# Pooling's doubling sums moved from GpSimd to VectorE, and the pooling units taken in reversed order

## The chip, the cores and the metric

The kernel runs on one core of a Trainium2 chip. The metric is the device time of one execution in microseconds (us). Lower is better. The engines are named as the profile names them: PE (TensorE's matmuls), PEld (TensorE's weight loads), DVE (VectorE), ACT (ScalarE), POOL (GpSimd), SP (SyncE, which issues DMAs).

## What is computed

One decoder layer, sequence 2048, width 1024, fp32. Two branches share one input projection `w_in` (six groups of 1024 columns: q, k, v, a gate, u, a second gate). The retention branch has 8 heads of 128. The pooling branch is a causal moving mean of u over a window, minus u itself, then a linear map per group, a scale and a gate. The 1024 pooled channels are four groups of 256 with windows 2, 4, 8 and 16:

```python
cs = jnp.cumsum(uf, axis=1)
for g, w in enumerate(POOL_WINDOWS):          # 2, 4, 8, 16
    cg = cs[..., sl]
    shifted = jnp.pad(cg, ((0, 0), (w, 0), (0, 0)))[:, :s]
    count = jnp.minimum(t + 1.0, float(w))[None, :, None]
    mixed = (cg - shifted) / count - uf[..., sl]
    outs.append(jnp.einsum('bsc,cd->bsd', mixed, pool_w[g]))
y_pool = concat(outs) * pool_scale * silu(g_pool)
```

Both branches are concatenated, mapped by `w_out`, normalised and added to x.

## The kernel before, in words

**Tiling.** Every large product is a 2x2 block product done the Strassen way, with seven products in place of eight. A "unit" is one such 2x2 problem with blocks of 128 output channels by 512 tokens. Each of its seven products is 12 matmuls of 128x512 (four slices of the contraction, three terms each, since operands are split into a rounded high part and a rest: `split`, L144 on ACT and L145 on DVE). The order of the products is 6, 2, 5, 7, then product 1 of the next unit, 4, 3. Three PSUM banks (a, b, c) hold the sums; bank b takes products 6, 7 and 4 in turn, and DVE or ACT must have read the bank after one of them before the next may add to it. So product 7 waits for the readers of product 6 (L340 on DVE, then the copy u at L315 on ACT), and product 4 waits for the reader of product 7 (L348 on DVE, called gp in a pooling unit).

**Phases.** `line` lists the units of four phases. Phase 0 does token blocks 0 and 1, phase 1 blocks 2 and 3; each has 24 units: a qk and a vg unit for each of the 8 heads and 8 pooling units `up0` to `up7` (two for each window: `g = f // 2`). `mixer_units` (L803) puts one pooling unit behind each head from head `lead` on (3 in phase 0, 2 in phase 1), and what is left at the end of the phase. Phases 2 and 3 are the output projection, 8 units each, first on the heads' half and then on the pooled half. At the end of a phase, `Resident.fetch` loads the next phase's moving operand and splits it: 14 copies `rh` of 128x1024 on ACT and 14 subtractions `rl` on DVE, within the last unit or two.

**Order of work.** The main loop emits one product, runs its readers (`uses`), then `slot()`, which runs what earlier stages have put there with `later(i, stage)` (i products ahead), then the chores of that point (`chores`, L1098), and the splits for the next unit (`prep`). The tile framework then orders each engine's instructions by its own plan; every engine runs its queue in order.

**The pooling unit** (`pool_unit`, L591). Product 2 gives u of the first block, 7 the gate of the second block, 4 the gate of the first, 3 u of the second. `values` writes u behind 16 columns of history into `ub`; `gate` applies SiLU on ACT. As soon as both are there (after product 4 for the first block, after product 3 for the second), `mix` runs whole: doubling sums (L631) on GpSimd, each adding a tile to itself shifted by 1, 2, 4, 8 (one sum for window 2, up to four for window 16), then on DVE the mean minus u (L634), for block 0 the first 16 columns once more (L638, L640), the scale and gate (L642), and a store by a DMA that GpSimd issues (`put_y`, L450). All this is emitted in the slot of the product that gave the last input.

`chores` also calls `fold_pool_weights(g)`, which multiplies the pooling weights of group g into the projection before the units of that group need them.

Of the kernel before, what the change touches and what calls it, by code (L numbers as in the profile page):

```python
# [13 lines left out]
ALU = mybir.AluOpType  # L14
# [4 lines left out]
KT = DM // P  # L19
KH = KT // 2  # L20
BLK = 512
# [8 lines left out]
HIST = 16  # L30
# [6 lines left out]
C_ID, C_TRI, C_G2, C_EPS, C_CNT, C_INVF, C_SGN, C_HPI = 0, 128, 256, 264, 272, 336, 337, 338  # L37
# [44 lines left out]
def layer_kernel(ctx: ExitStack, tc: tile.TileContext, x, xt, pos, wt, wut, wo, pw, cols, postg, const, out):  # L82
    nc = tc.nc
# [13 lines left out]
    cst = kp.tile([P, C_W], F32, name="cst")  # L97
    col = kp.tile([P, 3 * KT], F32, name="col")
# [20 lines left out]
    def T(name):  # L119
        return tmp.tile([P, BLK + HIST], F32, name=name, tag="t", bufs=NT)  # L120
# [34 lines left out]
    def later(i, stage):  # L155
        while len(slots) <= i:
            slots.append([])
        slots[i].append(stage)
# [290 lines left out]
    def put_y(b, f, t):  # L449
        nc.gpsimd.dma_start(out=yd[b][:, :, f, :], in_=t.rearrange("p (c t) -> p c t", c=CPB))  # L450
# [86 lines left out]
    def w_quads(f1, f2):  # L537
        lo, hi = slice(0, BLK), slice(BLK, 2 * BLK)
        return {"11": f1[:, lo], "12": f1[:, hi], "21": f2[:, lo], "22": f2[:, hi]}
# [54 lines left out]
    def pool_unit(f, b0, b1):  # L594
        g = f // 2
        win, E = WINDOWS[g], BLK + HIST
        sg, ub = {}, {}

        def gate(b):
            def use(c, i):  # L600
                t = T(f"gp{f}_{b}")[:, :BLK]
                if not i:
                    c(t)
                    c = t
                nc.scalar.activation(out=t, in_=c, func=AF.Silu)
                sg[b] = t
                mix(b)
            return use

        def values(b):  # L610
            def use(c, i):
                u = T(f"ub{f}_{b}")
                nc.scalar.copy(out=u[:, :HIST], in_=hist[f])
                if i:
                    nc.scalar.copy(out=u[:, HIST:], in_=c)
                else:
                    c(u[:, HIST:])
                nc.scalar.copy(out=hist[f], in_=u[:, BLK:])
                ub[b] = u
                mix(b)  # L620
            return use

        def mix(b):
            if b not in sg or b not in ub:
                return
            n, u = f"{f}_{b}", ub[b]
            src, step = u, 1
            while step < win:
                dst = T(f"w{n}_{step}")
                s0 = 2 * step - 1  # L630
                nc.gpsimd.tensor_tensor(out=dst[:, s0:], in0=src[:, s0:], in1=src[:, s0 - step:E - step], op=ALU.add)  # L631
                src, step = dst, 2 * step
            mx = T(f"mx{n}")[:, :BLK]
            nc.vector.scalar_tensor_tensor(out=mx, in0=src[:, HIST:], scalar=1.0 / win, in1=u[:, HIST:],  # L634
                                           op0=ALU.mult, op1=ALU.subtract)
            if b == 0:
                c0 = C_CNT + g * HIST
                nc.vector.tensor_tensor(out=mx[:, :HIST], in0=src[:, HIST:2 * HIST], in1=cst[:, c0:c0 + HIST],  # L638
                                        op=ALU.mult)
                nc.vector.tensor_tensor(out=mx[:, :HIST], in0=mx[:, :HIST], in1=u[:, HIST:2 * HIST],  # L640
                                        op=ALU.subtract)
            nc.vector.scalar_tensor_tensor(out=mx, in0=mx, scalar=col[:, 2 * KT + f:2 * KT + f + 1], in1=sg[b],  # L642
                                           op0=ALU.mult, op1=ALU.mult)
            put_y(b, KT + f, mx)

        return Unit(f"up{f}_{b0}", w_quads(wf[f], wt[4 * HEADS + f]),
                    {"11": values(b0), "12": values(b1), "21": gate(b0), "22": gate(b1)})
# [90 lines left out]
    def load_fold(g, dh):  # L738
        return [landing(f"wr{g}{dh}{ct}", wut[2 * g + dh][:, ct * BLK:(ct + 1) * BLK]) for ct in range(2)]

    def load_pool(g):
        return landing(f"pr{g}", pw[g])

    def halves(name, val):
        hi, lo = (T(f"{name}{k}")[:, :BLK] for k in "hl")
        split(hi, lo, val)
        return hi, lo

    def fold_split(g, dh, raw):
        return [halves(f"w{g}{dh}{ct}", raw[ct]) for ct in range(2)]  # L750

    def fold_products(g, dh, pool, w):
        phi, plo = pool
        sums = []
        for kk in range(2):
            o = rps(f"wf{g}_{dh}{kk}")
            for e in range(2):
                for ct in range(2):
                    whi, wlo = w[ct]
                    d0 = (2 * kk + e) * P  # L760
                    ds = slice(d0, d0 + P)
                    cs = slice(ct * 256, (ct + 1) * 256)
                    oe = o[:, e * 256:(e + 1) * 256]
                    nc.tensor.matmul(oe, r32(whi[:, ds]), r32(phi[:, cs]), start=(ct == 0), stop=False)
                    nc.tensor.matmul(oe, r32(whi[:, ds]), r32(plo[:, cs]), start=False, stop=False)
                    nc.tensor.matmul(oe, r32(wlo[:, ds]), r32(phi[:, cs]), start=False, stop=(ct == 1))
            sums.append(o)
        return sums

    def fold_store(g, dh, sums):  # L770
        fold = [T(f"wf{g}{j}{dh}")[:, :BLK] for j in range(2)]
        for kk, o in enumerate(sums):
            for j in range(2):
                nc.scalar.copy(out=fold[j][:, kk * 256:(kk + 1) * 256].rearrange("p (e c) -> p e c", e=2),
                               in_=o.rearrange("p (e c) -> p e c", e=2)[:, :, j * P:(j + 1) * P])
        for j in range(2):
            nc.gpsimd.dma_start(out=wf[2 * g + j][:, dh * BLK:(dh + 1) * BLK], in_=fold[j])

    def fold_pool_weights(g):
        st = {"pr": load_pool(g), 0: load_fold(g, 0)}  # L780

        def begin():
            st["p"] = halves(f"p{g}", st["pr"])

        def operands(dh):
            st[dh] = fold_split(g, dh, st[dh])

        def multiply(dh):
            st[dh] = fold_products(g, dh, st["p"], st[dh])

        def second():
            st[1] = load_fold(g, 1)
        later(2, begin)
        later(3, lambda: operands(0))
        later(6, lambda: multiply(0))
        later(7, lambda: fold_store(g, 0, st[0]))
        later(7, second)
        later(10, lambda: operands(1))
        later(13, lambda: multiply(1))
        later(14, lambda: fold_store(g, 1, st[1]))  # L800


    def mixer_units(b0, b1, lead):  # L803

        units = []
        pool = [pool_unit(f, b0, b1) for f in range(KT)]
        for h in range(HEADS):
            units += head_units(h, b0, b1)
            if h >= lead:
                units.append(pool.pop(0))  # L810
        return units + pool
# [259 lines left out]
    def stats_next(b):  # L1071
        ss = sml.tile([P, 2 * CPB], F32, name=f"ss{b}", tag="ss2", bufs=2)

        def rows(st):
            for j in range(2):
                t = T(f"xs{b}_{st}{j}")[:, :BLK]
                nc.sync.dma_start(out=t, in_=x[b * BLK + st * P:b * BLK + (st + 1) * P, j * BLK:(j + 1) * BLK])
                later(3, lambda t=t, j=j: nc.scalar.activation(out=t, in_=t, func=AF.Square,
                                                               accum_out=ss[:, 2 * st + j:2 * st + j + 1]))
        for st in range(CPB):  # L1080
            later(st, lambda st=st: rows(st))

        def scales():
            v = sml.tile([P, CPB], F32, name=f"rs{b}", tag="rs")
            s2 = ss.rearrange("p (s j) -> p s j", j=2)
            nc.vector.tensor_tensor(out=v, in0=s2[:, :, 0], in1=s2[:, :, 1], op=ALU.add)
            dg = diagonals(b, scale_h(b, v))
            later(2, lambda: spread_h(b, dg, True))
        later(9, scales)

    def postg_tiles():
        for j, tag in enumerate(("cos", "sin")):
# [2 lines left out]
            pg.append(t)  # L1095


    chores = {(0, 4, 0): lambda: fold_pool_weights(0), (0, 10, 0): lambda: fold_pool_weights(1),  # L1098
              (0, 14, 3): lambda: fold_pool_weights(2), (0, 16, 4): lambda: fold_pool_weights(3),
              (0, 6, 0): lambda: stats_next(2), (0, 7, 3): lambda: stats_next(3),  # L1100
              (0, 12, 1): lambda: tables(2), (0, 13, 2): lambda: tables(3),
              (0, last[0], 0): lambda: fetch_tables(2), (0, last[0], 1): lambda: fetch_tables(3),
# [9 lines left out]
    for n, (ph, i, u) in enumerate(line):  # L1112
# [5 lines left out]
        if after:  # L1118
            src = sources(ph + 1)
# [57 lines left out]
```

## Time and profile before

| | |
|---|---|
| median of 3 runs | 1507.88 us (1505.86 to 1511.87) |
| profiled execution, own time | 1509.98 us |
| profiled execution, span of the trace | 1508.0 us |
| mean granted TensorE clock | 0.985 |
| busy PE / DVE / ACT / POOL | 1436.5 / 1077.0 / 709.6 / 349.3 us |

Busy time is the sum over instructions of an engine; what it was not busy it waited. Stretches are given in us from the start of the span. Phase 0 ends and phase 1 begins at about 610 us, phase 1 gives way to phase 2 at about 1175 us, phase 2 to phase 3 at about 1330 us. "tail" below means the last pooling units of a phase, which stand one behind another.

### The profile page before, as it was taken

The page shows a single profiled execution, that of the slowest core. Times are in us where ns is not written, and L with a number is a line of the kernel's source. Part 1 is how long each engine was busy: PE and PEld are TensorE (multiplying, and loading weights), DVE is VectorE, ACT ScalarE, POOL GpSimd, SP SyncE. Part 2 cuts the span into 40 slices and gives each one's busy share as a digit, 9 for nine tenths or more (in the row PEclk, how much of TensorE's full clock was granted, in tenths as well). Part 3 has the DMA queues.
Part 4 walks back from the last instruction along what each step waited for, and adds up shares of the span by engine and source line. Part 5 has one row for each costly group of instructions (what it writes and reads, how often), then busy time and mean ns, then how long its engine had stood idle before and what let it go on. Part 6 is the DMA issues. An engine that isn't in the chain of part 4 may idle for free.

```text
span 1508.0 us, 20797 instructions
## 1 busy us (share of the span) xinstructions
PE 1436.5 (95%) x6976; PEld 1194.8 (79%) x6976; DVE 1077.0 (71%) x2280; ACT 709.6 (47%) x1353; POOL 349.3 (23%) x415
## 2 busy tenths in 40 slices
PE   5999999999999998999999999999998899998985
PEld 3888888888888876788888888888876788877874
DVE  7997677867866778776776768676767544576766
ACT  6464565555554434545444444443445433453321
POOL 0001012121302255310121213123135322112222
PEclk9999999999999999999999999999999999999998
DMA  8134365544545775643545635554537655798976
GB/s 335 32 95 123 107 177 149 162 139 107 159 114 152 226 219 184 204 112 92 147 139 140 162 96 156 138 152 137 155 86 224 202 152 153 220 289 212 235 219 166
DMA packets 115372, 243.79 MB, mean 162 GB/s; under 512 B 14016, under 2 KB 14144, under 8 KB 115264
## 3 DMA queue, kind: packets, MB, share of 16 engines
q1 hardware_dynamic: 79296, 156.46, 31.9%
q0 software_dynamic: 35968, 86.00, 25.3%
q8 instruction: 54, 0.88, 0.3%
q14 instruction: 54, 0.44, 0.1%
HBM read 187.88 MB, written 54.53 MB: 161 GB/s over the span
## 4 chain that ended last, share of the span: by engine, by line
PE 44%; DVE 5%; issue 5%; DMA 4%; POOL 3%; ACT 1%; SPq 1%; POOLq 0%; DVEq 0%; ACTq 0%
POOL w L631 2%; DMA S_o<-yd 2%; PE b_o L330 2%; PE b_o L331 2%; PE b_up L330 2%; PE b_o L332 2%; PE b_up L331 2%; PE b_up L332 2%; PE b_vg L332 1%; PE b_vg L330 1%; PE b_vg L331 1%; PE b_qk L330 1%; PE b_qk L331 1%; PE b_qk L332 1%; PE c_o L330 1%
## 5 line engine op out<-in xcount | busy, mean ns | idle before, releaser
L330 PE MATMUL b_up<-rh,h_up 128*128 128x512 f32 x192 | 78.6, 409 | 13.5 <-DVE gp L348 8.3
L330 PE MATMUL b_o<-rh,h_o 128*128 128x512 f32 x192 | 78.2, 407 | 13.5 <-DVE ot_o L348 9.2
L450 POOL DMA_DIRECT2D yd<-sg x32 | 24.7, 770 | 237.8 <-DVE sg L531 160.2
L331 PE MATMUL b_o<-rl,h_o 128*128 128x512 f32 x192 | 77.3, 403 | 0.0
L332 PE MATMUL b_up<-rh,l_up 128*128 128x512 f32 x192 | 77.0, 401 | 0.0
L331 PE MATMUL b_up<-rl,h_up 128*128 128x512 f32 x192 | 77.0, 401 | 0.0
L332 PE MATMUL b_o<-rh,l_o 128*128 128x512 f32 x192 | 76.9, 401 | 0.0
L330 PE MATMUL b_qk<-rh,h_qk 128*128 128x512 f32 x180 | 71.7, 398 | 3.1 <-ACT u_qk L315 2.5
L524 ACT ACTIVATE on<-op,sh,y_o 128x128 f32<-128x128 f32 x128 | 48.2, 457 | 51.5 <-DVE sh L521 51.5
L330 PE MATMUL b_vg<-rh,h_vg 128*128 128x512 f32 x180 | 72.0, 400 | 0.0
L331 PE MATMUL b_qk<-rl,h_qk 128*128 128x512 f32 x180 | 70.5, 392 | 0.8 <-DVE rl L145 0.6
L332 PE MATMUL b_qk<-rh,l_qk 128*128 128x512 f32 x180 | 70.4, 391 | 0.1
L331 PE MATMUL b_vg<-rl,h_vg 128*128 128x512 f32 x180 | 70.4, 391 | 0.0
L332 PE MATMUL b_vg<-rh,l_vg 128*128 128x512 f32 x180 | 70.4, 391 | 0.0
L263 POOL DMA_DIRECT2D S_qk<-in_wt x30 | 26.5, 907 | 174.0 <-DMA S_qk<-in_wt 114.6
L145 DVE TENSOR_TENSOR rl<-m,rh 128x1024 fp32r<-128x1024 f32 x42 | 53.0, 1265 | 19.1 <-ACT rh L144 16.4
L631 POOL TENSOR_TENSOR w<-w 128x525 f32<-128x525 f32 (+2 forms) x48 | 63.6, 1324 | 5.9 <-issue 2.8
L330 PEld LDWEIGHTS b_up<-rh,h_up 128*128 128x128 f32 x192 | 37.3, 194 | 24.5 <-DVE gp L348 10.0
L263 POOL DMA_DIRECT2D S_vg<-in_wt x30 | 26.6, 910 | 129.9 <-DMA S_vg<-in_wt 54.2
L330 PEld LDWEIGHTS b_o<-rh,h_o 128*128 128x128 f32 x192 | 37.5, 195 | 24.2 <-DVE ot_o L348 11.1
L330 PE MATMUL a_o<-rh,h_o 128*128 128x512 f32 x128 | 49.9, 390 | 2.8 <-ACT x_o L338 2.8
L631 POOL TENSOR_TENSOR w<-ub 128x527 f32<-128x527 f32 x32 | 44.0, 1374 | 35.9 <-DVE ub L354 15.2
(498 smaller groups left out, 4675.5 us busy)
## 6 DMA issues: line engine op xcount, KB each, us to landing
m<-made SPq DMA_DIRECT2D x30, 512.0 KB, 5.5
made<-c POOLq DMA_DIRECT2D x48, 256.0 KB, 3.3
yd<-sg POOLq DMA_DIRECT2D x32, 256.0 KB, 2.7
S_up<-in_wt POOLq DMA_DIRECT2D x32, 256.0 KB, 6.1
yd<-mx POOLq DMA_DIRECT2D x32, 256.0 KB, 2.9
b<-in_wo SPq DMA_DIRECT2D x32, 256.0 KB, 4.0
S_o<-yd SPq DMA_DIRECT2D x32, 256.0 KB, 3.4
S_o<-yd POOLq DMA_DIRECT2D x32, 256.0 KB, 7.2
```

What stands on the lines that cost most here:

```text
L145: (eng or nc.vector).tensor_tensor(out=r32(lo), in0=val, in1=hi, op=ALU.subtract)
L263: nc.gpsimd.dma_start(out=dst, in_=self.quads[more], accum_op=ALU.add)
L330: nc.tensor.matmul(o, wh, mh, start=opens and j == 0, stop=False, **more)
L331: nc.tensor.matmul(o, wh, ml, start=False, stop=False, **more)
L332: nc.tensor.matmul(o, wl, mh, start=False, stop=j == KH - 1, **more)
L450: nc.gpsimd.dma_start(out=yd[b][:, :, f, :], in_=t.rearrange("p (c t) -> p c t", c=CPB))
L524: nc.scalar.activation(out=self.on[:, c], in_=op[:, c], func=AF.Identity, scale=rs[:, i:i + 1], bias=shift[:, i:i + 1])
L631: nc.gpsimd.tensor_tensor(out=dst[:, s0:], in0=src[:, s0:], in1=src[:, s0 - step:E - step], op=ALU.add)
```

## The change

The doubling sums go to DVE, one stage each through `later(0, ...)`, so that they run in the slot behind the product that gave the last input; the rest of `mix` becomes `finish`, put one product later with `later(1, ...)`. The sums are otherwise the same instructions on the same tiles. The pooling units are taken in the order f = 7 to 0, and the chores fold the weights of the groups in the order 3, 2, 1, 0 at the same four points.

```diff
             n, u = f"{f}_{b}", ub[b]
-            src, step = u, 1
+            cur, step = [u], 1
+
+            def widen(step):
+                src, dst = cur[0], T(f"w{n}_{step}")
+                s0 = 2 * step - 1
+                nc.vector.tensor_tensor(out=dst[:, s0:], in0=src[:, s0:], in1=src[:, s0 - step:E - step], op=ALU.add)
+                cur[0] = dst
+
+            def finish():
+                src, mx = cur[0], T(f"mx{n}")[:, :BLK]
...
+                put_y(b, KT + f, mx)
             while step < win:
-                dst = T(f"w{n}_{step}")
-                s0 = 2 * step - 1
-                nc.gpsimd.tensor_tensor(out=dst[:, s0:], in0=src[:, s0:], in1=src[:, s0 - step:E - step], op=ALU.add)
-                src, step = dst, 2 * step
...
+                later(0, lambda step=step: widen(step))
+                step *= 2
+            later(1, finish)
...
-        pool = [pool_unit(f, b0, b1) for f in range(KT)]
+        pool = [pool_unit(f, b0, b1) for f in reversed(range(KT))]
...
-    chores = {(0, 4, 0): lambda: fold_pool_weights(0), (0, 10, 0): lambda: fold_pool_weights(1),
-              (0, 14, 3): lambda: fold_pool_weights(2), (0, 16, 4): lambda: fold_pool_weights(3),
+    chores = {(0, 4, 0): lambda: fold_pool_weights(3), (0, 10, 0): lambda: fold_pool_weights(2),
+              (0, 14, 3): lambda: fold_pool_weights(1), (0, 16, 4): lambda: fold_pool_weights(0),
```

## Rows read from the trace of the kernel before

**Rows 1.** The page: busy time of each engine.

```profile
PE 1436.5 (95%) x6976; PEld 1194.8 (79%) x6976; DVE 1077.0 (71%) x2280; ACT 709.6 (47%) x1353; POOL 349.3 (23%) x415
```

**Rows 2.** Busy time by stretch: PE, PEld, DVE, ACT, POOL, granted clock, DMA, GB/s.

```profile
520.00:640.00 120.00, 109.44 (x474) 86.94 (x473) 98.16 (x149) 56.74 (x106) 60.10 (x62) 0.96 0.66 195
920.00:940.00 20.00, 19.34 (x91) 15.65 (x90) 18.34 (x31) 11.52 (x21) 4.73 (x7) 1.00 0.60 163
1040.00:1060.00 20.00, 18.50 (x84) 14.98 (x83) 13.77 (x27) 8.46 (x19) 9.22 (x9) 1.00 0.53 152
1100.00:1200.00 100.00, 87.96 (x377) 70.40 (x377) 68.70 (x101) 46.13 (x83) 45.71 (x43) 0.95 0.61 182
1320.00:1340.00 20.00, 17.22 (x77) 13.91 (x76) 14.68 (x19) 10.32 (x16) 2.87 (x4) 1.00 0.92 313
240.00:300.00 60.00, 60.00 (x299) 50.33 (x298) 48.51 (x119) 27.50 (x52) 13.66 (x18) 1.00 0.61 167
260.00:280.00 20.00, 20.00 (x94) 16.33 (x93) 19.56 (x33) 12.12 (x21) 5.67 (x9) 1.00 0.72 201
```

**Rows 3.** TensorE's waits, 540 to 640 us: for whom, us, times, longest.

```profile
PE b_up L330 <- DVE gp L348: 4.6, 3, 3.6
PE b_up L330 <- ACT u_up L315: 3.5, 2, 2.4
```

**Rows 4.** TensorE's waits, 1100 to 1200 us.

```profile
PE b_o L330 <- ACT u_o L315: 4.3, 1, 4.3
PE b_up L330 <- DVE gp L348: 3.6, 1, 3.6
```

**Rows 5.** VectorE's waits, 540 to 640 us.

```profile
DVE mx L634 <- POOL w L631: 8.2, 6, 2.3
```

**Rows 6.** VectorE's waits, 1100 to 1200 us.

```profile
DVE mx L634 <- POOL w L631: 11.0, 5, 4.6
```

**Rows 7.** GpSimd's largest group of doubling sums: count, busy, mean ns.

```profile
L631 POOL TENSOR_TENSOR w<-ub 128x527 f32<-128x527 f32 x32 | 44.0, 1374 | 35.9 <-DVE ub L354 15.2 <-DVE mx L638 7.6 <-DVE w111l L145 7.4
```

**Rows 8.** TensorE in order of time, 600 to 606 us.

```profile
601.45 0.63 PE L331 MATMUL b_up<-rl,h_up 128*128 128x512 f32 x1
...
605.72 0.63 PE L332 MATMUL b_up<-rh,l_up 128*128 128x512 f32 x1
```

**Rows 9.** TensorE in order of time, 564 to 567 us.

```profile
564.24 0.39 PE L330 MATMUL a_up<-b21h,h_up 128*128 128x512 f32 x1
...
566.96 0.39 PE L330 MATMUL c_up<-rh,h_up 128*128 128x512 f32 x1
```

**Rows 10.** VectorE in order of time, 280 to 283 us.

```profile
280.90 0.69 DVE L145 TENSOR_TENSOR l_up<-11_up,h_up 128x512 fp32r<-128x512 f32 x1
281.50 0.69 DVE L281 TENSOR_TENSOR sS_up<-S_up,11_up 128x512 f32<-128x512 f32 x1
282.23 0.69 DVE L281 TENSOR_TENSOR sS_up<-sS_up,12_up 128x512 f32<-128x512 f32 x1
```

**Rows 11.** VectorE in order of time, 591 to 594 us.

```profile
591.75 2.13 DVE L281 TENSOR_TENSOR sS_qk<-S_qk,11_qk 128x512 f32<-128x512 f32 x1
```

**Rows 12.** GpSimd in order of time, 588 to 594 us.

```profile
588.76 2.52 POOL L631 TENSOR_TENSOR w<-w 128x525 f32<-128x525 f32 x2
...
591.96 1.36 POOL L631 TENSOR_TENSOR w<-w 128x513 f32<-128x513 f32 x1
```

**Rows 13.** VectorE, around phase 2 to 3: product 7's reader at L348.

```profile
1296.98 0.69 DVE L348 TENSOR_TENSOR pt_o<-b_o,x_o 128x512 f32<-128x512 f32 x1 [1.63 <-PE b_o L332]
...
1316.02 0.69 DVE L348 TENSOR_TENSOR pt_o<-b_o,x_o 128x512 f32<-128x512 f32 x1 [1.14 <-PE b_o L332]
...
1341.72 0.68 DVE L348 TENSOR_TENSOR ot_o<-b_o,x_o 128x512 f32<-128x512 f32 x1
...
1359.01 0.69 DVE L348 TENSOR_TENSOR ot_o<-b_o,x_o 128x512 f32<-128x512 f32 x1
```

**Rows 14.** VectorE's subtractions for the next phase's operand.

```profile
L145 DVE TENSOR_TENSOR rl<-m,rh 128x1024 fp32r<-128x1024 f32 x42 | 53.0, 1265 | 19.1 <-ACT rh L144 16.4 <-PE a_up L331 1.2 <-PE a_o L331 1.2
```

More of the change, by code (lines that the diff above doesn't have):

```diff
@@ L626, in mix @@
             n, u = f"{f}_{b}", ub[b]
-            src, step = u, 1
-            while step < win:
-                dst = T(f"w{n}_{step}")
-                s0 = 2 * step - 1
-                nc.gpsimd.tensor_tensor(out=dst[:, s0:], in0=src[:, s0:], in1=src[:, s0 - step:E - step], op=ALU.add)
-                src, step = dst, 2 * step
-            mx = T(f"mx{n}")[:, :BLK]
-            nc.vector.scalar_tensor_tensor(out=mx, in0=src[:, HIST:], scalar=1.0 / win, in1=u[:, HIST:],
-                                           op0=ALU.mult, op1=ALU.subtract)
@@ L636, in mix @@
[L636 to L643, printed above, removed]
@@ L644, in mix @@
-            put_y(b, KT + f, mx)
+            cur, step = [u], 1
[6 more added lines that the diff above has]
+                src, mx = cur[0], T(f"mx{n}")[:, :BLK]
+                nc.vector.scalar_tensor_tensor(out=mx, in0=src[:, HIST:], scalar=1.0 / win, in1=u[:, HIST:],
+                                               op0=ALU.mult, op1=ALU.subtract)
+                if b == 0:
+                    c0 = C_CNT + g * HIST
+                    nc.vector.tensor_tensor(out=mx[:, :HIST], in0=src[:, HIST:2 * HIST], in1=cst[:, c0:c0 + HIST],
+                                            op=ALU.mult)
+                    nc.vector.tensor_tensor(out=mx[:, :HIST], in0=mx[:, :HIST], in1=u[:, HIST:2 * HIST],
+                                            op=ALU.subtract)
+                nc.vector.scalar_tensor_tensor(out=mx, in0=mx, scalar=col[:, 2 * KT + f:2 * KT + f + 1], in1=sg[b],
+                                               op0=ALU.mult, op1=ALU.mult)
+                put_y(b, KT + f, mx)
```

## The prediction, made before the change was run

> **What bounds the kernel now.** I read the page first. PE is busy 1436.5 of 1508.0 us [rows 1], so all that any change off PE can win is some 71 us of idle time, plus what PE loses at the lower clock. The table by stretches then shows where that time lies: PE works without a gap through nearly all of phases 0 and 1 and loses time where a phase's last pooling units follow one another. In 520 to 640 us PE is busy 109.44 of 120 us, in 1100 to 1200 us 87.96 of 100 [rows 2]: 10.6 and 12.0 us idle. Single gaps of 0.7 and 1.5 us lie at 920 to 940 and 1040 to 1060 us [rows 2]. The rest is the start and phase 3, which the change does not touch.
>
> The waits say what ends the idle time. In both tails PE waits for DVE's reader of product 7 (gp) and for the copy behind DVE's reader of product 6 (u) [rows 3, 4]. Nobody there lacks weights: PE waits because DVE is late at reading a bank. And DVE is late, among other things, because it stands in its queue until GpSimd has made a doubling sum: 8.2 us in the first tail and 11.0 us in the second [rows 5, 6]. GpSimd's largest group of these sums has a mean of 1374 ns [rows 7], and in the old order the tails hold the longest chains: f = 5, 6, 7 (3, 4 and 4 sums for each of two blocks, 22) and f = 6, 7 (16).
>
> After the longest idle times the matmuls run at the lower of the two clock levels: 11 of them start from 601.45 to 605.72 us, 0.427 us apart [rows 8], where 13 start from 564.24 to 566.96 us, 0.227 apart [rows 9]. I count 20 such matmuls in the first tail and 15 in the second: 35 x 0.2 = 7.0 us. The tails lose 10.6 + 12.0 + 7.0 = 29.6 us in all.
>
> **The change part by part.**
>
> The sums on DVE: 80 instructions (two units for each of four windows, four blocks, 1 to 4 sums). No row shows such a sum on DVE; the nearest are additions of two SBUF tiles at L281, as large within 3%. One that depends on the addition ahead of it starts 0.73 us after it, one with other work ahead 0.60 [rows 10]. So a sum takes 0.60 to 0.73 us of the queue; since a chain's sums depend on one another I take 0.70: 80 x 0.70 = 56 us on an engine that is idle for 431 us [rows 1]. Most of this is hidden: 240 to 300 us holds the first pooled unit, with DVE busy 48.5 of 60 us and PE without a gap [rows 2]; in the new order that unit (f = 7) adds 2 x 4 x 0.70 = 5.6 us there, 54.1 of 60. [...]
>
> The tails: f = 2, 1, 0 now stand at the end of phase 0 (2 + 1 + 1 sums, two blocks: 8) and f = 1, 0 at the end of phase 1 (4). 12 x 0.70 = 8.4 us on DVE take the place of 19.2 us of waiting. The change also ends a second loss: while GpSimd adds, DVE's own additions stretch. One at L281 took 2.13 us [rows 11], where its like take 0.69 [rows 10], and GpSimd was adding for most of that time [rows 12]. I give this no term of its own: both are why DVE is late, and the idle time of PE is counted once.
>
> What is late next: the handover. At the end of a phase DVE also makes 14 subtractions `rl` of 1.265 us [rows 14], 17.7 us in about one unit. From phase 2 to 3 the same handover takes place with no pooling beside it: PE idles 2.8 us in 1320 to 1340 [rows 2], and the reader of product 7, elsewhere 19.04 us apart, comes 25.70 and then 17.29 us later, 4.9 us over two units [rows 13]. So a tail keeps 2.8 to 4.9 us; DVE has more to do in a pooling unit than in an output unit, but PE's idle time is what counts, so I take the middle, 3.85, twice: 7.7 us. Gain in the tails: 29.6 - 7.7 = 21.9 us.
>
> The single gaps (2.2 us) go to heavier chains: their places held f = 2 and 4 and now hold f = 5 and 3, and f = 7 to 4, with 4 and 3 sums, stand between the heads. A chain of four holds DVE for 2.8 us, a product lasts 12 x 0.227 = 2.72, and bank b's readers have one product (gp) or two (u) of slack. I bound this from a gain of 2.2 to a loss of 4.4 and take zero, since the stretch at 240 to 300 us has room.
>
> `finish` one product later: two instructions of DVE (four in block 0) move behind the next product's reader, which shortens DVE's queue ahead of that reader. The store goes with them, one of GpSimd's issues for each block; it is not read until phase 3, more than 150 us after the last pooling unit. u, the gate and the last sum stay in their buffers some 2.7 us longer; before, GpSimd's slower chains held them as long, so I cost that at nothing, at most one more wait of a product. GpSimd's queue loses its sums, so its accumulating loads stand behind less. The folding chores come at the same four points with the same work: zero.
>
> Sum: 21.9 us off. The profiled execution took 1509.98 us, 2.1 above the median of the runs, so 1509.98 - 21.9 = 1488.1 for it and 1507.88 - 21.9 = **1486.0** for the median.
>
> **The rivals.**
>
> A: only the waits for GpSimd go, and DVE stays the limit of the tails. Then the gain is 19.2 - 8.4 = 10.8 us: 1497.1. For it: DVE is busy 98 of 120 us in the first tail [rows 2]. Against it: part of that is stretched additions.
>
> B: the handover binds the tails. Phase 2 to 3 has one interval of 25.70 us in place of 19.04, 6.66 us longer [rows 13], without any pooling. If two units in each tail go on losing that, 26.6 of 29.6 us stay: 1504.9, no change that can be seen. Against it: PE lost only 2.8 us there.
>
> C, slower: DVE becomes the bound between the heads. It decides where DVE lags PE by more than the two products of slack (5.4 us) as a chain starts; from there on every chain shows on PE in full. f = 7, 6 make 8 chains of 2.8 us and f = 5, 4 make 8 of 2.1: 39.2 us lost against 21.9 won, 1525.2. For it: DVE is busy 19.56 of 20 us in 260 to 280, right behind the first pooled unit [rows 2]. Against it: PE never paused there.
>
> D: the change doesn't do what it says: the framework plans the sums or `finish` ahead of the readers after all, and DVE is as late as before; within 0.5%.
>
> **How the numbers follow.** Forecast 0.64, A 0.14, B 0.10, C 0.08, D 0.04. About 0.5% (7.5 us) is what a measurement of this kernel can tell from no change. Faster by more: forecast and A, 0.78. Same: B and D, 0.14. Slower: C, 0.08. The range starts at the whole of the tails and gaps won, 29.6 + 2.2 = 31.8 us, 1476, less 2 for the spread of the runs: 1474. It ends at 1503, past A, short of B; B, C and part of D, about 0.2, are outside. The forecast's own range is 1474 to 1494.
>
> **What would show it.** Right: no wait of DVE at L634 for another engine; sums of 0.6 to 0.75 us on DVE; both tails with under 6 us of idle PE each and no matmuls 0.43 us apart; GpSimd some 110 us less busy (80 sums of about 1.374). Wrong: gp and u still head PE's waits in the tails (A or B, told apart by whether `rl` stands ahead of gp); new waits of PE for L340 or L348 behind f = 7 to 4 (C); sums standing ahead of the readers in DVE's order (D).

## The result and the profile after

The changed kernel takes 1476.28 us (median of 4 runs, 1475.41 to 1479.11) against 1508.63 of the kernel before in the same comparison: the ratio is 0.9781, with a 95% interval of 0.9765 to 0.9797. The forecast was 1486.0 with a range of 1474 to 1503: the direction and the place were right; the gain of 32.35 us is half as much again as the 21.9 us forecast and lies near the fast end of the range.

The page's busy times after the change (it answers to [rows 1]):

```profile
PE 1423.2 (97%) x6976; PEld 1188.4 (81%) x6976; DVE 1085.0 (74%) x2360; ACT 712.3 (48%) x1353; POOL 249.1 (17%) x335
```

PE idles 51.3 us where it idled 71.5. DVE has 80 instructions more and is busy only 8.0 us longer; the next sections turn on that. GpSimd is busy 100.2 us less, where some 110 were forecast.

The table by stretches after the change (columns as in [rows 2]; the second row is the last pooling units of phase 1 and the handover, at their new times):

```profile
520.00:640.00 120.00, 119.74 (x570) 99.39 (x569) 104.02 (x188) 66.83 (x122) 25.82 (x36) 1.00 0.72 216
1080.00:1180.00 100.00, 98.29 (x440) 79.83 (x439) 71.20 (x118) 51.52 (x91) 19.48 (x26) 1.00 0.71 208
240.00:300.00 60.00, 59.72 (x295) 49.54 (x294) 51.25 (x125) 27.55 (x51) 11.34 (x16) 1.00 0.59 167
```

The reader is to compare the second number of a row with the first. The tail of phase 0 lost 10.6 us of PE before [rows 2] and loses 0.3 now; that of phase 1 lost 12.0 and loses 1.7. (The 0.3 lies at 520 to 540 us and stood there before as well.) Both stretches show a granted clock of 1.00 where it was 0.96 and 0.95. The stretch of the first pooled unit, now with chains of four, loses 0.3 us.

What PE still waits for from 500 to 1340 us, phase 2 and its handover included (it answers to [rows 3, 4]; two rows of 0.3 us follow these):

```profile
PE a_o L330 <- ACT x_o L338: 2.6, 1, 2.6
PE c_o L330 <- ACT rh L144: 0.8, 1, 0.8
PE b_o L331 <- DVE rl L145: 0.7, 2, 0.4
```

Neither gp nor u stands there any more; what is left are splits of the next phase's operand (`rl`, `rh`) and 2.6 us for a copy at the handover from phase 2 to 3, which has no pooling.

**Where the time came from.** One instruction serves as a mark in both traces: DVE's reader of product 7 in the first unit of the tail of phase 0, in the first unit of phase 1 and in the second unit of phase 2. Before:

```profile
529.66 0.69 DVE L348 TENSOR_TENSOR gp<-b_up,x_up 128x512 f32<-128x512 f32 x1 [0.94 <-PE b_up L332]
...
625.88 0.69 DVE L348 TENSOR_TENSOR rot_k<-b_qk,x_qk 128x512 f32<-128x512 f32 x1
```

and, of the same view later on,

```profile
1201.79 0.69 DVE L348 TENSOR_TENSOR pt_o<-b_o,x_o 128x512 f32<-128x512 f32 x1 [1.63 <-PE b_o L332]
```

After:

```profile
529.54 0.69 DVE L348 TENSOR_TENSOR gp<-b_up,x_up 128x512 f32<-128x512 f32 x1 [0.94 <-PE b_up L332]
...
608.68 0.68 DVE L348 TENSOR_TENSOR rot_k<-b_qk,x_qk 128x512 f32<-128x512 f32 x1
```

and

```profile
1167.86 0.69 DVE L348 TENSOR_TENSOR pt_o<-b_o,x_o 128x512 f32<-128x512 f32 x1 [1.61 <-PE b_o L332]
```

The kernels are level up to 529.6 us, within 0.1. Over the tail of phase 0 the changed one gains 17.1 us (96.2 became 79.1), by the second unit of phase 2 another 16.7 (33.9 in all, with the 0.1), and of the span it keeps 33.5.

The table by stretches from the first mark to the last, before and then after (columns as in [rows 2]):

```profile
529.66:1201.79 672.13, 647.52 (x3146) 537.36 (x3145) 493.42 (x1003) 314.79 (x591) 194.67 (x215) 0.98 0.54 152
```

```profile
529.54:1167.86 638.32, 636.40 (x3145) 532.74 (x3145) 492.56 (x1055) 317.03 (x591) 108.47 (x147) 1.00 0.56 160
```

The same matmuls are done in both. PE idles 24.6 us of the first and 1.9 of the second, 22.7 less; it is busy 11.1 us less, in part because matmuls at the lower clock last longer (0.63 us in [rows 8], 0.39 in [rows 9]) and count as busy. Together that is the 33.8 us.

### The profile page after: what moved, and what is told of

The parts are those of the page before. It is cut to its first block, busy times and chain, and to the rows that moved or that the text cites. A ratio compares the mean times of both kernels' runs of the same rounds, so it can differ in the third digit from the quotient of the medians.

```text
span 1474.5 us, 20756 instructions
## 1 busy us (share of the span) xinstructions
PE 1423.2 (97%) x6976; PEld 1188.4 (81%) x6976; DVE 1085.0 (74%) x2360; ACT 712.3 (48%) x1353; POOL 249.1 (17%) x335
## 5 line engine op out<-in xcount | busy, mean ns | idle before, releaser
L330 PE MATMUL b_up<-rh,h_up 128*128 128x512 f32 x192 | 75.5, 393 | 0.0
L145 DVE TENSOR_TENSOR rl<-m,rh 128x1024 fp32r<-128x1024 f32 x42 | 51.1, 1223 | 19.6 <-ACT rh L144 15.5
L144 ACT CAST rh<-m 128x1024 fp32r<-128x1024 f32 x42 | 43.7, 1048 | 15.7 <-DMA m<-made 8.4
L330 PE MATMUL c_o<-rh,h_o 128*128 128x512 f32 x128 | 50.3, 393 | 0.8 <-ACT rh L144 0.8
L331 PE MATMUL c_o<-rl,h_o 128*128 128x512 f32 x128 | 50.1, 392 | 0.3 <-DVE rl L145 0.3
L332 PE MATMUL c_o<-rh,l_o 128*128 128x512 f32 x128 | 49.8, 389 | 0.0
```

The source lines that it names most:

```text
L144: nc.scalar.copy(out=r32(hi), in_=val)
L145: (eng or nc.vector).tensor_tensor(out=r32(lo), in0=val, in1=hi, op=ALU.subtract)
L330: nc.tensor.matmul(o, wh, mh, start=opens and j == 0, stop=False, **more)
L331: nc.tensor.matmul(o, wh, ml, start=False, stop=False, **more)
L332: nc.tensor.matmul(o, wl, mh, start=False, stop=j == KH - 1, **more)
```

## The experiments

The theory (the "engine theory" of the texts below): GpSimd's sums held DVE, by making it wait and by stretching DVE's own additions, and the engine is what counts. The rivals: the long chains only hurt beside the handover, so the order is what counts; or mixing one product later is.

### Each part of the change, alone and together

Four runs at first. `e1_reversed_only`:

```diff
-        pool = [pool_unit(f, b0, b1) for f in range(KT)]
+        pool = [pool_unit(f, b0, b1) for f in reversed(range(KT))]
...
-    chores = {(0, 4, 0): lambda: fold_pool_weights(0), (0, 10, 0): lambda: fold_pool_weights(1),
+    chores = {(0, 4, 0): lambda: fold_pool_weights(3), (0, 10, 0): lambda: fold_pool_weights(2),
...
```

> The kernel before with the pooling units reversed and nothing else: the sums stay on GpSimd, mixing stays whole. Engine theory (DVE is held by GpSimd's sums, by waiting and by stretched additions, and the engine is what counts): the tails' chains shrink from 22 and 16 sums to 8 and 4 but still hold DVE, and chains of four stand between the heads; 1488 to 1500 us. Order theory (the long chains only hurt beside the handover): nearly all of the gain, 1476 to 1484 us. If the order is worth nothing: 1505 us or more.

`e2_dve_only`:

```diff
-                nc.gpsimd.tensor_tensor(out=dst[:, s0:], in0=src[:, s0:], in1=src[:, s0 - step:E - step], op=ALU.add)
+                nc.vector.tensor_tensor(out=dst[:, s0:], in0=src[:, s0:], in1=src[:, s0 - step:E - step], op=ALU.add)
```

> The kernel before with the sums on DVE, mixing whole and at once, pooling units in the old order. Engine theory: 38 sums of 0.7 us in the tails take the place of 19.2 us of waiting and of the stretched additions, so most of the gain is there, 1478 to 1486 us. Order theory: with chains of four beside the handover DVE is as full as before, 1494 us or more.

`e3_dve_later_old_order`, against the changed kernel (with the chores back in the old order as well):

```diff
-        pool = [pool_unit(f, b0, b1) for f in reversed(range(KT))]
+        pool = [pool_unit(f, b0, b1) for f in range(KT)]
```

> The changed kernel with the pooling units in the old order (sums on DVE and both stages put later). Engine theory: 1476 to 1484 us, within 4 us of the run with the sums on DVE and mixing at once; if the later stages carry the gain, this one is more than 8 us faster than that one. Order theory: 1490 us or more.

`e4_gpsimd_later_reversed`, against the changed kernel:

```diff
-                nc.vector.tensor_tensor(out=dst[:, s0:], in0=src[:, s0:], in1=src[:, s0 - step:E - step], op=ALU.add)
+                nc.gpsimd.tensor_tensor(out=dst[:, s0:], in0=src[:, s0:], in1=src[:, s0 - step:E - step], op=ALU.add)
```

> The changed kernel with the sums put back on GpSimd: reversed order and both stages put later stay. If DVE's waiting was the loss, mixing one product later hides most of it: 1477 to 1484 us. If the stretching of DVE's own additions beside GpSimd's counts as well, it stays: 1486 to 1498 us.

Their outcomes left open which of the two stages works and whether it matters in the reversed order. Four more filled the table. `e5_finish_at_once`, against the changed kernel:

```diff
-            later(1, finish)
+            later(0, finish)
```

> The changed kernel with mixing in the same slot as the sums (one product earlier). My costing gave the later mixing nothing: 1474 to 1479 us, the same as the changed kernel. If the later mixing keeps the readers of the banks on time, PE waits again for L348 or L340 and the time is 1482 us or more.

`e8_old_order_at_once` makes the same edit in the kernel of `e3_dve_later_old_order`:

```diff
-            later(1, finish)
+            later(0, finish)
```

> Sums on DVE in the slot, mixing in the same slot, pooling units in the old order. Between the run with mixing whole (1499 us) and the one with mixing a product later (1487 us): if the later mixing carries those 12 us, 1495 to 1502; if what carries them is that the sums leave the product's own readers for the slot, 1484 to 1490.

`e9_dve_reversed_no_stages` makes the edits of the first two runs together in the kernel before:

```diff
-        pool = [pool_unit(f, b0, b1) for f in range(KT)]
+        pool = [pool_unit(f, b0, b1) for f in reversed(range(KT))]
...
-                nc.gpsimd.tensor_tensor(out=dst[:, s0:], in0=src[:, s0:], in1=src[:, s0 - step:E - step], op=ALU.add)
+                nc.vector.tensor_tensor(out=dst[:, s0:], in0=src[:, s0:], in1=src[:, s0 - step:E - step], op=ALU.add)
```

> Sums on DVE, pooling units reversed, mixing whole and at once as before the change. If order and stages do the same work twice (each keeps DVE free at the handover), 1475 to 1481 us; if the stages count by themselves as in the old order, 1484 us or more.

`e11_gpsimd_later_old_order`, against the kernel of `e3_dve_later_old_order`:

```diff
-                nc.vector.tensor_tensor(out=dst[:, s0:], in0=src[:, s0:], in1=src[:, s0 - step:E - step], op=ALU.add)
+                nc.gpsimd.tensor_tensor(out=dst[:, s0:], in0=src[:, s0:], in1=src[:, s0 - step:E - step], op=ALU.add)
```

> The kernel before with both stages put later and nothing else (sums on GpSimd, old order). The reversed order with the same stages ran 1505 us. Stretching theory: the stages hide waiting and leave the stretching, 1498 to 1508 us. Waiting theory: 1480 to 1492 us.

Measured, as medians in us, with the ratio to the kernel before and its interval:

| sums, mixing | old order | reversed order |
|---|---|---|
| GpSimd, whole at once | the kernel before, 1 | 1507.98, 0.9996 (0.9982 to 1.001) |
| GpSimd, mixing a product later | 1500.72, 0.9941 (0.9921 to 0.9962) | 1505.38, 0.9989 (0.9974 to 1.0003) |
| DVE, whole at once | 1499.35, 0.9948 (0.9932 to 0.9964) | 1479.11, 0.9801 (0.977 to 0.9832) |
| DVE, both stages in one slot | 1500.26, 0.9932 (0.9906 to 0.9957) | 1476.74, 0.9787 (0.9767 to 0.9806) |
| DVE, mixing a product later | 1487.02, 0.9868 (0.9851 to 0.9885) | the changed kernel, 1476.28, 0.9781 |

Of the expectations, `e1_reversed_only` and `e2_dve_only` came out on the far side from the engine theory (the order alone is worth nothing; the engine alone is slower than 1494 us), `e3_dve_later_old_order` between the ranges of both theories, and `e4_gpsimd_later_reversed` above both of its ranges. The second four came out in one of their ranges each: `e5_finish_at_once` with nothing for the later mixing, `e8_old_order_at_once` with the later mixing carrying the gain, `e9_dve_reversed_no_stages` with order and stages doing the same work twice, `e11_gpsimd_later_old_order` where the stretching theory had put it.

My theory missed in its plain form: the engine alone gives 9 us, not 22 to 30, and the order alone gives nothing, yet the two together give all but some 3 us, which the intervals of 0.9801 and 0.9781 do not tell apart. Neither part adds to the other; each takes away what spoils the other. The traces show how.

The order alone moves the loss. The table by stretches of `e1_reversed_only`:

```profile
260.00:280.00 20.00, 14.31 (x51) 10.43 (x50) 14.31 (x23) 6.22 (x12) 8.05 (x8) 0.83 0.45 145
340.00:360.00 20.00, 16.85 (x69) 13.50 (x69) 17.58 (x28) 9.95 (x20) 9.90 (x10) 0.91 0.50 146
540.00:640.00 100.00, 98.62 (x447) 80.58 (x446) 87.13 (x146) 55.40 (x100) 41.63 (x44) 1.00 0.78 238
780.00:800.00 20.00, 17.55 (x68) 13.44 (x67) 19.21 (x27) 7.80 (x16) 11.23 (x13) 0.91 0.43 141
...
1100.00:1200.00 100.00, 99.36 (x461) 82.08 (x460) 75.15 (x131) 52.94 (x97) 27.11 (x31) 1.00 0.63 193
```

The tails are nearly whole (1.4 and 0.6 us lost). But at 260 to 280 us, where the kernel before never paused [rows 2], 5.7 us are lost, 3.2 at 340 and 2.5 at 780, with a granted clock of 0.83 and 0.91: the chains of four now stand there, on GpSimd. The 5.7 us are one wait of PE for an instruction of a chore (`dg`, L376; 22.5 us in two waits, of which the other has 16.8) that stands in DVE's queue behind the mean of such a chain.

The engine alone keeps the chains of four at the handover. PE's waits in `e2_dve_only`:

```profile
PE a_o L332 <- DVE l_o L145: 9.0, 2, 7.3
PE a_vg L332 <- DVE l_vg L145: 5.9, 1, 5.9
PE a_qk L332 <- DVE l_qk L145: 3.4, 2, 2.3
```

The two handovers of the same run by stretch:

```profile
580.00:640.00 60.00, 51.04 (x214) 40.41 (x213) 54.37 (x81) 33.18 (x54) 6.60 (x8) 0.91 0.65 197
1120.00:1180.00 60.00, 51.03 (x216) 41.12 (x215) 50.54 (x69) 32.46 (x52) 9.85 (x14) 0.94 0.77 233
```

PE loses 9.0 us in each, now because splits (L145) come late: in DVE's queue they stand behind four sums, the mixing and the subtractions `rl`. With the mixing a product later (`e3_dve_later_old_order`) the same stretches lose 4.8 and 3.3, and those waits all but go there (0.5 us is left; one of 3.0 for a copy and one of 1.8 for a reader of product 7 take their place):

```profile
580.00:640.00 60.00, 55.17 (x252) 44.89 (x251) 56.17 (x87) 36.49 (x59) 8.32 (x10) 0.97 0.69 204
1120.00:1180.00 60.00, 56.75 (x242) 45.92 (x241) 50.84 (x71) 32.54 (x54) 11.64 (x16) 0.97 0.78 247
```

So the later mixing is worth 10 us by the ratios and 13 by the medians where chains are long at the handover (1500.26 against 1487.02), and nothing that can be seen where they are short (1476.74 against 1476.28).

### What GpSimd's sums cost DVE

In `e4_gpsimd_later_reversed` DVE's waits for the sums fell to these two rows, 13.0 us, from 24.5 us in all in the kernel before and 21.1 in `e1_reversed_only`, which has the same order; and the time did not move clear of zero:

```profile
DVE mx L637 <- POOL w L632: 8.9, 5, 3.8
...
DVE ub L354 <- POOL w L632: 4.1, 1, 4.1
```

This does not yet tell waiting from stretching. With the same 2280 instructions DVE's busy time rose as its waits fell, from 1079.5 us in `e1_reversed_only` to 1089.7:

```profile
PE 1432.5 (95%) x6976; PEld 1192.1 (79%) x6976; DVE 1089.7 (73%) x2280; ACT 710.2 (47%) x1353; POOL 345.6 (23%) x415
```

What DVE no longer waits for a sum, it is stretched by sums: the time lost to GpSimd stays about the same. In the old order (`e11_gpsimd_later_old_order`) it is alike, 10.6 us of waits and 1086.3 us busy, but there the time falls by 8 us.

To cost the stretching alone, GpSimd must add where nobody waits for it. The first try, `e6_idle_gpsimd_sums`, computes what the changed kernel computes and besides adds slices of a constant tile:

```diff
+    ghost = kp.tile([P, 264], F32, name="ghost")
...
+                for _ in range(2):
+                    nc.gpsimd.tensor_tensor(out=ghost, in0=cst[:, 64:328], in1=cst[:, 63:327], op=ALU.add)
```

> The changed kernel, and beside each sum on DVE GpSimd makes two additions of 264 columns that nobody reads, about as much work as the sum it had before. Nothing waits for them, so what they cost is the stretching of DVE's additions alone (and the delay of GpSimd's own DMA issues). If waiting was the loss: 1474 to 1481 us. If stretching was a good part of it: 1483 to 1492 us, with DVE's busy time up by 15 us or more.

1550.01 us, ratio 1.0266 (1.0249 to 1.0283), and no answer: with no input to wait for, the additions were planned at the start of the kernel. GpSimd is busy 8 or 9 tenths of the first four slices, its accumulating loads come behind that, and PE waits 40.9 us for one copy. The page's row of GpSimd over 40 slices, and then the row of PE's waits:

```profile
POOL 8999111021111122211012121211111222212222
```

```profile
PE b_qk L331 <- ACT h_qk L145: 40.9, 1, 40.9
```

`e10_gpsimd_adds_beside` ties each addition to the sum it stands beside:

```diff
+    ghost = kp.tile([P, 400], F32, name="ghost")
...
+                nc.gpsimd.tensor_tensor(out=ghost, in0=dst[:, 128:], in1=dst[:, 128:], op=ALU.add)
```

> The changed kernel, and behind each sum on DVE GpSimd adds 400 columns of its result into a tile that nobody reads, so that the additions stand where the sums stood and nothing of DVE waits for their results. Stretching theory: DVE's busy time rises by 25 to 50 us and most of the gain goes, 1494 to 1525 us. Waiting theory (GpSimd's sums cost only what DVE waits for them): 1474 to 1482 us, DVE's busy time up by less than 10.

1503.09 us, ratio 0.9961 (0.9941 to 0.9981): 27 of the 32 us are gone again. The page's busy times:

```profile
PE 1432.0 (96%) x6976; PEld 1190.6 (79%) x6976; DVE 1115.5 (74%) x2360; ACT 711.1 (47%) x1353; POOL 333.9 (22%) x415
```

The group of GpSimd's additions:

```profile
L634 POOL TENSOR_TENSOR ghost<-w 128x400 f32<-128x400 f32 x80 | 87.5, 1094 | 73.1 <-DVE w L633 63.1 <-DVE mx L643 8.0 <-DVE mx L645 0.8
```

One group of DVE's sums:

```profile
L633 DVE TENSOR_TENSOR w<-w 128x521 f32<-128x521 f32 x16 | 16.2, 1014 | 0.0
```

DVE has the same 2360 instructions as in the changed kernel and is busy 30.5 us longer; a sum of 521 columns takes 1014 ns there where it takes 694 in the changed kernel:

```profile
L632 DVE TENSOR_TENSOR w<-w 128x521 f32<-128x521 f32 x16 | 11.1, 694 | 0.0
```

DVE waits for none of these additions. (GpSimd also holds the sums' buffers longer in this run, and its DMA issues stand behind the additions; the waits of DVE and PE show no sign that this counts, but it was not tried apart.)

Two more runs put plain instructions in place of the stretching. `e7_sums_twice` and `e12_48_more_sums` issue all sums, and all but the first of each chain, twice on DVE:

```diff
                 nc.vector.tensor_tensor(out=dst[:, s0:], in0=src[:, s0:], in1=src[:, s0 - step:E - step], op=ALU.add)
+                nc.vector.tensor_tensor(out=dst[:, s0:], in0=src[:, s0:], in1=src[:, s0 - step:E - step], op=ALU.add)
```

> The changed kernel with each sum issued twice on DVE, 80 more instructions of 0.7 us, 56 us of DVE. If DVE between the heads is near its bound (the slower rival), chains of eight sums (5.6 us against 2.7 us of a product) show on PE: 8 chains of 2.8 us or more, 1498 us or more. If the slack there is as I costed it, 1476 to 1484 us.

```diff
-                nc.vector.tensor_tensor(out=dst[:, s0:], in0=src[:, s0:], in1=src[:, s0 - step:E - step], op=ALU.add)
+                for _ in range(1 if step == 1 else 2):
+                    nc.vector.tensor_tensor(out=dst[:, s0:], in0=src[:, s0:], in1=src[:, s0 - step:E - step], op=ALU.add)
```

> The changed kernel with the second and later sums of a chain issued twice on DVE: 48 more sums, 48 x 0.70 = 33.6 us of DVE, about the 30.5 us by which GpSimd's additions beside the sums had raised DVE's busy time, and nothing on GpSimd. If that run's 27 us were DVE's lost time, whatever it was lost to: 1496 to 1508 us. If stretching costs more than the DVE time it takes (by delaying single readers): 1488 us or less.

The busy times of the first of the two:

```profile
PE 1436.5 (94%) x6976; PEld 1193.3 (78%) x6976; DVE 1135.1 (75%) x2440; ACT 710.5 (47%) x1353; POOL 249.2 (16%) x335
```

and of the second:

```profile
PE 1433.8 (95%) x6976; PEld 1191.7 (79%) x6976; DVE 1114.9 (74%) x2408; ACT 711.0 (47%) x1353; POOL 248.5 (17%) x335
```

All sums twice: 1525.32 us, ratio 1.0105 (1.0086 to 1.0124), slower than the kernel before; DVE is busy 50.1 us longer than in the changed kernel, and 49 us of that come out as time. 48 sums twice: 1503.71 us, ratio 0.996 (0.994 to 0.998), DVE busy 29.9 us longer, 27.4 us of time. That is the run with GpSimd's additions over again (30.5 us of DVE, 26.8 of time): at these places what counts is DVE's time, whatever it is lost to.

This also gives a budget of the change, as an estimate. 80 more sums raised DVE's busy time by 50.1 us; if the first 80 cost as much, DVE works 1085.0 - 50.1 = 1034.9 us without them. The kernel before shows 1077.0 [rows 1]: 42.1 us of it were stretching, and 24.5 more were waiting. The instructions bear this out one by one: 50 of DVE's that overlap a sum of GpSimd before the change last longer than their like after it, by 39 us together. The change spends 50.1 us of DVE and gets 66.6 back, 16.5 net.

The budget alone does not give the 32 us. With sums on DVE and mixing at once, DVE is busy nearly as long in the old order (`e2_dve_only`, the first row) as in the reversed one (`e9_dve_reversed_no_stages`, the second):

```profile
PE 1428.0 (95%) x6976; PEld 1192.3 (80%) x6976; DVE 1087.8 (73%) x2360; ACT 711.8 (48%) x1353; POOL 249.0 (17%) x335
```

```profile
PE 1425.4 (97%) x6976; PEld 1189.9 (81%) x6976; DVE 1086.2 (74%) x2360; ACT 712.1 (48%) x1353; POOL 248.7 (17%) x335
```

Yet the second is 20 us faster: where DVE's time falls due counts as well, and that is what the order changes.

## Why the prediction was right, and where it was off

**Right:** the place (both tails, bank readers late on DVE), the signs to look for (no wait of L637 for another engine, sums of 688 to 701 ns, no gp or u among PE's waits), the sums' size (0.70 taken; 50.1 / 80 = 0.63 of busy time measured on the sums of `e7_sums_twice`).

**The kept loss of the handovers** (7.7 us taken, from 2.8 to 4.9 each) measured 1.7 in all, beside the 0.3 that the change does not touch. The upper end was a misreading: the interval of 25.70 us between two readers of product 7 [rows 13] was taken as lost time. After the change the handover from phase 2 to 3 still has the like interval (1282.11 to 1307.62 us), with PE idle for 2.6: a late reader is no loss while PE has another product to do. The lower end does not carry over either: the pooled tail of phase 0 keeps nothing.

**The clock's term** (7.0 us, 35 matmuls counted) held as far as it goes: between the marks 34 matmuls last 0.6 us or more before and none after. But PE is busy 11.1 us less there; the other 4.1 are not explained. (The mean granted clock, 0.04 x 120 + 0.05 x 100 = 9.8 us, is no measure of it, since the clock is low while PE idles, too: from 1152.60 to 1159.40 us it is 0.50, and PE is busy 3.34 of these 6.80 us.)

**The single gaps against the heavier chains**, taken as zero, are a gain of 2.2: both gaps are gone and the chains of four cost next to nothing (0.3 us in the first). So PE's idle time gave 22.7 us where 10.6 + 12.0 - 7.7 = 14.9 were forecast, and its busy time 11.1 where 7.0 were: 33.8 in place of 21.9. The place and the mechanism there were right; the forecast fell short first by the loss kept at the handovers, 6.0 of the 11.9 us.

**"I give this no term of its own"** is the step whose reason fell short. It set stretching beside waiting as two causes of one loss and costed the exchange in the tails by the waits, 19.2 against 8.4. The stretching was the larger of the two, 42.1 against 24.5 us by the estimate above. It also bears on **"most of this is hidden"**, since DVE is idle for 431 us. The 80 sums were hidden: PE loses 0.3 us at the first pooled unit. But DVE's busy time there rose by 2.7 us (48.5 to 51.25 of 60) where the prediction added 5.6, and in all by 8.0. By the budget above the sums took the room that GpSimd's had taken up before. That the idle time would have done as well is not shown, and the next 50 us of sums at the same places cost 49. What the first 80 would cost against a kernel without any, no run shows.

**Rival C** was nearer than its 0.08 says. Its price (39.2 us for chains of four and three between the heads) is of the size of what the doubled sums pay (49 us), and they pay at the places it named. `e7_sums_twice` by stretch, PE losing 6.5 and 7.0 us behind the first pooled unit of each phase:

```profile
260.00:280.00 20.00, 13.52 (x47) 10.08 (x46) 17.41 (x29) 7.11 (x13) 5.02 (x7) 0.83 0.56 159
...
800.00:820.00 20.00, 13.01 (x50) 9.99 (x49) 16.90 (x27) 7.71 (x13) 4.02 (x6) 0.83 0.69 197
```

The change itself shows nothing of this kind, and it raises DVE's busy time by only 8.0 us where the doubled sums raise it by 50.1 more. Rivals A, B and D fell: both tails are freed, and gp is on time.

**The order** I costed only by the chains' lengths in the tails. The runs show that it is worth nothing with the sums on GpSimd at once (0.9996) and some 20 us with the sums on DVE at once (1499.35 against 1479.11).

## What to carry to other kernels

Before moving work between DVE and GpSimd, compare the durations of DVE's own instructions inside and outside the time that GpSimd computes: here the stretching was an estimated 42.1 us against 24.5 of waits for the sums, and it stood under DVE's busy time, not under its idle time. The idle time of an engine whose instructions are due at fixed points need not be slack (DVE idles 389.5 us in the changed kernel, and 50.1 us more of its work cost 49); adding a known dose of work at the place in question and reading the time tells how much is left there. Two edits that each show nothing or little can need each other, so a part that fails alone is tried again with the others in place.

## What the runs showed of the hardware

How far GpSimd stretches DVE's short instructions was not expected. Durations of two lines before, as minimum, median and maximum in ns. L640 subtracts 16 columns, both inputs from SBUF:

```profile
L640 DVE TENSOR_TENSOR mx<-mx,ub x8: 169/392/1042, 256.2 to 613.9; 128x16 f32<-128x16 f32 x8
```

The four of these that overlap a sum of GpSimd took 609 to 1042 ns, the other four 169 to 176. L340 has one input in PSUM:

```profile
L340 DVE TENSOR_TENSOR b_up<-b_up,x_up x16: 684/698/700, 232.3 to 1144.4; 128x512 f32<-128x512 f32 x16
```

Both kinds in order of time, while GpSimd makes two sums from 588.76 to 591.28 us [rows 12]:

```profile
588.75 1.62 DVE L642 SCALAR_TENSOR_TENSOR mx<-mx,col,gp 128x512 f32<-128x512 f32 x1
590.29 0.68 DVE L340 TENSOR_TENSOR b_up<-b_up,x_up 128x512 f32<-128x512 f32 x1
```

The subtraction of L640 after the change, now L643:

```profile
L643 DVE TENSOR_TENSOR mx<-mx,ub x8: 161/167/169, 256.8 to 596.1; 128x16 f32<-128x16 f32 x8
```

A subtraction of 16 columns took up to 1042 ns beside GpSimd's sums and at most 169 ns in the kernel without them. L642, with its inputs in SBUF, took 1.62 us in that stretch (its median is 0.745), while the reader of PSUM (L340), wholly inside a sum, took 0.68. The addition of [rows 11] starts 0.21 us ahead of GpSimd's sum [rows 12] and is stretched all the same, to 2.13 us. An instruction with a single tile as input was stretched as well: `y_o` (L134), a TENSOR_SCALAR of 4 columns with a median of 170 ns, took up to 1916 ns, and that longest one, from 905.02 us, overlaps a sum of GpSimd from 905.28 to 906.90 us. What decides which instruction is stretched no run shows. By the budget above the stretching came to an estimated 42.1 us.

80 more sums, which last 685 to 701 ns each in `e7_sums_twice`, raised DVE's busy time by 50.1 us, 0.63 us each. That is less than they last: a sum can start before the one ahead has ended, as in [rows 10], where an instruction of 0.69 us is followed by the next 0.60 us after its start.
